# Holding the first products of the first gate stage in text order, and giving stored half tiles back later

## The chip, the cores and the metric

The kernel runs on one core of a Trainium2 chip. TensorE multiplies matrices into PSUM banks; VectorE and ScalarE do the elementwise work; GpSimd does a little of it and issues the stores of intermediate results; SyncE issues loads. Each engine works through its own list of instructions in order and waits at an instruction until what it depends on is done. The metric is the device time of one execution in microseconds (us); lower is better.

## The reference

One decoder layer with two recurrent branches on the same normalised input. For the change only its end matters: each branch output is projected, weighted by a sigmoid gate that comes from the input projection, and the sum goes through one output projection.

```python
proj = h @ w_in[l]
hq, hf, hi, hz, gq, gk, gv, gz, ga, mg = jnp.split(proj, IN_OFFSETS, axis=-1)
y_h = hgrn2_branch(hq, hf, hi, hz, lb_all[l], hgrn_norm_w[l])
y_g = gla_branch(gq, gk, gv, gz, ga, gla_alpha_w[l], gla_alpha_b[l], gla_norm_w[l])
u_h = y_h @ w_branch[l, 0]
u_g = y_g @ w_branch[l, 1]
mg = jax.nn.sigmoid(mg.reshape(B, T, N_BRANCH, D_MODEL))
merged = mg[:, :, 0] * u_h + mg[:, :, 1] * u_g
x = x + gate[:, None, :] * (merged @ w_out[l])
```

All of it is float32, 1024 rows by 1024 columns for `h`, each gate and each `u`.

## The kernel before

**The last stages.** The two gate projections and the two branch projections are four weight blocks b: 0 is the gate of the second branch (its sigmoid is `gate1`), 1 the other gate, 2 and 3 the branch projections. Each 1024 x 1024 product is cut into 2 x 2 blocks and computed with seven products of sums of blocks instead of eight (Strassen's way), in the order p = 1, 2, 5, 3, 6, 7, 4 (`PRODUCTS`). A product has four pairs i = 0 to 3 (two 128-row output tiles each), and for each pair `Pair.run` issues 12 matmuls (line 1343): four slices kt of the inner dimension times three terms n, since each float32 operand is split into a high and a low part. (b,p) i below is one such run. Its result stands in a PSUM bank of 512 columns.

**What each run needs and leaves.** The operands: a raw tile is loaded by SyncE (weights L1274 and L1278, inputs L1230), ScalarE makes the high part (L1285 for weights, L1263 or L1260 for inputs) and VectorE the low part (L1286, L1264, L1261). W(b,p,j) stands for the weights of pairs 2j and 2j+1, H(b,p) for the input side. After a run, `Pair.after` copies or combines banks: L1317 and L1315 copy a bank to a half tile in SBUF (`snap_of`), L1323 copies one back (`seed`), L1330 adds a copy and a bank on VectorE (`summed`), and `outs[b]` puts the finished half tile away. For b = 0 that is `put_gate1`: a sigmoid on ScalarE (L1414) and a store to DRAM on GpSimd (L1415); the gate is loaded again in the last two blocks. A new run into a bank waits for the copy that empties it.

**Slots.** All tiles of the last stages live in 46 slots of SBUF. `Slots` hands out the slot that has been free longest. `Halves` (called `Q`) cuts a slot into two halves of 128 x 512; a free half of a slot that is already open goes first. A tile that gets a slot waits until all that was done with its last owner is over, a store included.

**What sets the order.** Inside some stretches the order of instructions is the text's. Elsewhere, and in the whole of the stretch that the change touches, a list scheduler of the framework orders each engine's instructions by what depends on what and by its estimates; `tc.keep_in_program_order(m)` ties an instruction to the one ahead of it on its engine in the text. The first gate stage (b = 0) lies where the recurrent branches finish (L683 to L967: scores, decays, norms), so TensorE's rows of both are mixed.

Of the kernel before, what the change touches and what calls it, by code (L numbers as in the profile page):

```python
# [83 lines left out]
def hybrid_trunk_kernel(  # L84
# [6 lines left out]
    nc = tc.nc  # L91
# [10 lines left out]
    Q = Halves(S)  # L102
# [35 lines left out]
    def load_x(t):  # L138
        b = S.get([D])
        nc.sync.dma_start(b, x2[t * P:(t + 1) * P, :])  # L140
        return b
# [357 lines left out]
    for n in (1, 4):  # L499
        m = cp.tile([P, 8 // n, 6, n], F32, name=f"mask{n}")  # L500
# [6 lines left out]
    m = cp.tile([P, 1, 16], F32, name="mask16")  # L507
# [39 lines left out]
    class Feat:  # L547
# [12 lines left out]
        def run(self):  # L560
            ps = dtile()
            yield from mm_feat(self.wt, self.rhs, ps, self.w)
            S.free(*self.wt)
            self.done(ps)
# [742 lines left out]
    class Pair:  # L1307
# [25 lines left out]
        def run(self, p):  # L1333
            if p in (1, 5):
                self.bank[BANK[p]] = R.get()
            o = self.bank[BANK[p]]
            hi, lo = (z[:, self.i % 2, :] for z in wt[self.b, p, self.i // 2])
            h = H[0 if self.b == 1 else self.b, p]
            for kt in range(4):
                h_hi, h_lo = (z[kt // 2][:, kt % 2, :] for z in h)  # L1340
                sl = slice(kt * P, (kt + 1) * P)
                for n, (a, c) in enumerate(((hi, h_hi), (hi, h_lo), (lo, h_hi))):
                    nc.tensor.matmul(o, a[:, sl], c, start=(p in (1, 5) and kt == 0 and n == 0),  # L1343
                                     stop=(kt == 3 and n == 2), skip_group_check=True)
                if kt % 2:
                    stream.weave(1)
            if self.i % 2:
                S.free(*wt.pop((self.b, p, self.i // 2)))

        def after(self, p):  # L1350
            bank, snap, out = self.bank, self.snap, outs[self.b]
            if p == 1:
                if self.b:
                    self.seed()
                else:
                    snap[1] = self.snap_of("a", -1.0)
            elif p == 2:
                out(2 * self.i, 0, bank["a"], False)
                R.free(bank.pop("a"))
            elif p == 5:  # L1360
                snap[5] = self.snap_of("e")
            elif p == 6:
                snap[6] = self.snap_of("b", -1.0)
                self.summed(0, 1, None, bank["e"], ALU.subtract, 6)
                R.free(bank.pop("e"))
            elif p == 7:
                self.summed(1, 1, bank["b"], None, ALU.add, 5)
            elif p == 4:
                out(2 * self.i + 1, 0, bank["b"], False)
                R.free(bank.pop("b"))  # L1370
# [41 lines left out]
    def put_gate1(d, half, ap, summed):  # L1412
        g = ap if summed else Q.get()
        nc.scalar.activation(g, ap, AF.Sigmoid)  # L1414
        nc.gpsimd.dma_start(gate1_d[d][:, half * 512:half * 512 + 512], g)  # L1415
        Q.free(g)

    def put_gate0(d, half, ap, summed):
        nc.scalar.activation(merged(d, half), ap, AF.Sigmoid)
# [13 lines left out]
    def put_m(d, half, ap, summed):  # L1433
# [5 lines left out]
        if d % 2 != half:  # L1439
            S.free(gate1.pop(d))  # L1440

    outs[:] = [put_gate1, put_gate0, put_t1, put_m]


# [5 lines left out]
    for g in BUILT[1:]:  # L1450
        n = GROUPS.index(g)
# [53 lines left out]
    def load_rows(*ts):  # L1505
        for t in ts:
            xr[t] = load_x(t)

    bank4, snap4 = {}, {}

    def out_run(p, i):
# [141 lines left out]
    for b in (2, 3):  # L1653
        for p, i, z in ((3, 3, "11"), (6, 1, "21"), (6, 3, "12"), (7, 2, "22")):
            after(b - 1, p, i, lambda b=b, z=z: load_quad(b, z))
            if b == 3:
                p, i = {(3, 3): (7, 2), (6, 1): (7, 3), (6, 3): (4, 2), (7, 2): (4, 3)}[p, i]
# [61 lines left out]
```

## Time and profile before

| | |
|---|---|
| median of 3 runs | 1216.99 us (1215.41 to 1218.84) |
| profiled execution | 1216.46 us, span 1214.8 us |
| TensorE busy | 1184.1 us, 97% |
| VectorE, ScalarE, GpSimd busy | 65%, 45%, 10% |
| granted TensorE clock | 0.998 |
| first gate stage | about 806 to 900 us of the span |

The profile gives one execution on the chip. Its views used below: the page with the engines' busy shares; a table of busy time by stretches; each engine's own line of time (start, length, engine, line, tiles, count, and in brackets the idle time before the row and what ended it); the DMA groups with the time from issue to landing. Matmuls are pipelined: the length of a row of many says more than that of one. PE is TensorE, DVE is VectorE, ACT is ScalarE, POOL is GpSimd, SP or SPq is SyncE.

### The profile page before, as it was taken

How to read it: one execution, taken by the hardware profiler on the slowest of the kernel's cores; microseconds unless marked ns; L12 is line 12 of the kernel's file. 1: busy time of each engine (PE TensorE's matmuls, PEld its weight loads, DVE VectorE, ACT ScalarE, POOL GpSimd, SP SyncE). 2: the span in 40 equal slices, each digit the busy share in tenths (PEclk: the TensorE clock that was granted, in tenths of full speed). 3: DMA queues.
4: the chain of work that ended last, by engine and by line, in shares of the span. 5: the costliest groups of instructions: out<-in, count | busy, mean ns of one | idle time of the engine just before them, and what ended most of it. 6: DMA issues, size and time to landing. Idle time of an engine off the chain costs nothing.

```text
span 1214.8 us, 20860 instructions
## 1 busy us (share of the span) xinstructions
PE 1184.1 (97%) x8579; PEld 982.6 (81%) x8579; DVE 790.9 (65%) x1245; ACT 546.9 (45%) x797; POOL 123.8 (10%) x215
## 2 busy tenths in 40 slices
PE   5999999999999999999999999999999999999997
PEld 3777889889798888888887888877778888878886
DVE  4637444774848456877884365794653775988994
ACT  5646732434434244344332324455743544444554
POOL 4100000202111121121110101011220000000000
PEclk9999999999999999999999999999999999999999
DMA  9814000844444267255341112054697746435523
GB/s 320 277 70 139 18 19 19 293 141 161 156 152 149 66 207 249 94 179 169 108 174 47 59 53 70 36 174 158 227 343 277 260 160 208 135 104 173 174 104 122
DMA packets 130961, 183.51 MB, mean 151 GB/s; under 512 B 7467, under 2 KB 97633, under 8 KB 130866
## 3 DMA queue, kind: packets, MB, share of 16 engines
q1 hardware_dynamic: 117250, 136.87, 35.7%
q0 software_dynamic: 13568, 45.31, 9.6%
q8 instruction: 67, 1.10, 0.4%
q14 instruction: 28, 0.23, 0.1%
q10 hardware_dynamic: 48, 0.01, 0.0%
HBM read 132.87 MB, written 49.28 MB: 150 GB/s over the span
## 4 chain that ended last, share of the span: by engine, by line
PE 61%; issue 23%; DVE 3%; ACT 3%; POOL 2%; DMA 1%; POOLq 0%; ACTq 0%; DVEq 0%
PE pd L541 19%; PE pd L1343 9%; PE sc_ps L1343 5%; PE pm L1343 5%; PE pd L1520 3%; PE pd L643 2%; PE pd L644 2%; PE pd L645 2%; PE sc_ps L1520 2%; PE pm L848 1%; PE pd L352 1%; PE pm L829 1%; PE pm L850 1%; PE pm L1520 1%; PE sc_ps L352 1%
## 5 line engine op out<-in xcount | busy, mean ns | idle before, releaser
L541 PE MATMUL pd<-b,b 128*128 128x512 f32 x1632 | 387.4, 394 | 0.0
L541 PEld LDWEIGHTS pd<-b,b 128*128 128x128 f32 x1632 | 302.4, 188 | 64.8 <-issue 1.4
L1343 PE MATMUL pd<-b,b 128*128 128x512 f32 x720 | 173.7, 392 | 4.3 <-ACT b L1414 2.1
L1343 PEld LDWEIGHTS pd<-b,b 128*128 128x128 f32 x720 | 133.7, 188 | 35.7 <-ACT b L1414 3.2
L197 DVE TENSOR_TENSOR b<-b,b 128x1024 fp32r<-128x1024 f32 (+2 forms) x89 | 98.9, 1122 | 83.1 <-ACT b L196 65.4
L196 ACT CAST b<-b 128x1024 fp32r<-128x1024 f32 (+2 forms) x89 | 82.9, 948 | 92.1 <-DVE b L1199 14.6
L1286 DVE TENSOR_TENSOR b<-b,b 128x1024 fp32r<-128x1024 f32 x56 | 68.3, 1224 | 66.9 <-ACT b L1285 52.3
L1285 ACT CAST b<-b 128x1024 fp32r<-128x1024 f32 x56 | 58.3, 1050 | 73.9 <-PE pd L1343 20.6
L1343 PE MATMUL sc_ps<-b,b 128*128 128x512 f32 x324 | 79.4, 391 | 1.0 <-ACT scT L793 1.0
L600 PE MATMUL pd<-b,b 128*128 128x256 f32 x256 | 74.2, 290 | 0.0
L1264 DVE TENSOR_TENSOR b<-b,b 128x1024 fp32r<-128x1024 f32 x48 | 59.2, 1251 | 20.8 <-ACT b L1263 15.1
L602 PE MATMUL pd<-b,b 128*128 128x256 f32 x256 | 72.5, 283 | 0.0
L601 PE MATMUL pd<-b,b 128*128 128x256 f32 x256 | 72.4, 283 | 0.0
L1343 PEld LDWEIGHTS sc_ps<-b,b 128*128 128x128 f32 x324 | 60.3, 188 | 14.6 <-ACT scT L793 1.4
L1343 PE MATMUL pm<-b,b 128*128 128x512 f32 x300 | 72.1, 389 | 0.0
L1263 ACT CAST b<-b 128x1024 fp32r<-128x1024 f32 x48 | 49.9, 1050 | 41.2 <-PE pd L1343 16.0
L1343 PEld LDWEIGHTS pm<-b,b 128*128 128x128 f32 x300 | 56.3, 188 | 11.7
L352 PE MATMUL pd<-b,b 128*128 128x512 f32 x192 | 53.3, 410 | 2.0 <-ACT b L196 0.9
L1201 POOL DMA_DIRECT2D ws<-b x64 | 34.6, 541 | 192.0 <-DVE b L1195 86.5
L735 ACT COPY xb<-b 128x512 f32<-128x512 f32 x48 | 29.4, 620 | 49.4 <-PE sc_ps L715 26.7
L643 PE MATMUL pd<-b,b 128*128 128x512 f32 x128 | 51.3, 401 | 0.0
L644 PE MATMUL pd<-b,b 128*128 128x512 f32 x128 | 50.0, 390 | 0.0
(285 smaller groups left out, 1964.3 us busy)
## 6 DMA issues: line engine op xcount, KB each, us to landing
b<-in_w_in_dram SPq DMA_DIRECT2D x66, 512.0 KB, 4.2
ws<-b POOLq DMA_DIRECT2D x64, 256.0 KB, 3.3
b<-ws SPq DMA_DIRECT2D x32, 512.0 KB, 4.9
b<-in_x_dram SPq DMA_DIRECT2D x16, 512.0 KB, 5.7
b<-in_ada_w_dram SPq DMA_DIRECT2D x32, 256.0 KB, 6.9
b<-in_w_branch_dram SPq DMA_DIRECT2D x16, 512.0 KB, 4.4
b<-h SPq DMA_DIRECT2D x14, 512.0 KB, 4.3
wo<-b POOLq DMA_DIRECT2D x14, 512.0 KB, 5.7
```

What stands on the lines that cost most here:

```text
L196: nc.scalar.copy(hi, src)
L197: nc.vector.tensor_sub(lo, src, hi.bitcast(F32))
L352: nc.tensor.matmul(accs[f], wg(a, d, f), b[d][:, half * 512:half * 512 + 512], start=(d == 0 and n == 0), stop=(d == KT - 1 and n == 2))
L541: nc.tensor.matmul(ps[0:w, th * 512:(th + 1) * 512], a[:, k, 0:w], b[:, th * 512:(th + 1) * 512], start=(k == 0 and n == 0), stop=(k == KT ...
L600: nc.tensor.matmul(o, lh, hi[:, k % 4, :], start=(k == 0), stop=False)
L601: nc.tensor.matmul(o, lh, lo[:, k % 4, :], start=False, stop=False)
L602: nc.tensor.matmul(o, ll, hi[:, k % 4, :], start=False, stop=(k == KT - 1))
L643: nc.tensor.matmul(o, lh, hi[:, k % 2, :], start=(k == 0), stop=False)
L644: nc.tensor.matmul(o, lh, lo[:, k % 2, :], start=False, stop=False)
L1286: nc.vector.tensor_sub(lo, t, hi.bitcast(F32))
L1343: nc.tensor.matmul(o, a[:, sl], c, start=(p in (1, 5) and kt == 0 and n == 0), stop=(kt == 3 and n == 2), skip_group_check=True)
L1520: nc.tensor.matmul(o, a, b, start=(p in (1, 5) and kt == 0 and n == 0), stop=(kt == 3 and n == 2), skip_group_check=True)
```

## The change

For b = 0 and p = 1, the first matmul of each pair is tied to the matmul ahead of it in the text. And a half tile that `put_gate1` has stored is not freed at once: it goes into a list, and is freed when three newer ones stand behind it; the last three are freed after the run (1,2) i0.

```diff
@@ Pair.run
-                    nc.tensor.matmul(o, a[:, sl], c, start=(p in (1, 5) and kt == 0 and n == 0),
-                                     stop=(kt == 3 and n == 2), skip_group_check=True)
+                    m = nc.tensor.matmul(o, a[:, sl], c, start=(p in (1, 5) and kt == 0 and n == 0),
+                                         stop=(kt == 3 and n == 2), skip_group_check=True)
+                    if (self.b, p) == (0, 1) and kt == 0 and n == 0:
+                        tc.keep_in_program_order(m)
@@ put_gate1
         nc.gpsimd.dma_start(gate1_d[d][:, half * 512:half * 512 + 512], g)
-        Q.free(g)
+        sent.append(g)
+        drop_sent(3)
+
+    sent = deque()
+
+    def drop_sent(leave):
+        while len(sent) > leave:
+            Q.free(sent.popleft())
@@ ahead of the output stage
+    after(1, 2, 0, lambda: drop_sent(0))
```

Lines behind the first addition stand two further down in the new kernel, those behind the second nine and more: the sigmoid L1414 is L1416 there, the gate store L1415 is L1417.

The lists of instructions show what the scheduler makes of it; names of buffers carry a number. On TensorE, in (0,1), `pd_7440` is the bank of i0 and i1, `pd_7441` that of i2 and i3. What stood between i0 and i1:

```order
 L1343 MATMUL pd_7440<-b_7395,b_7404 128x512
 L1343 MATMUL pd_7440<-b_7393,b_7405 128x512
-L1343 MATMUL pd_7441<-b_7392,b_7442 128x512
-L1343 MATMUL pd_7441<-b_7394,b_7442 128x512
-L1343 MATMUL pd_7441<-b_7392,b_7443 128x512
-L1343 MATMUL pd_7441<-b_7392,b_7442 128x512
 L1343 MATMUL pd_7440<-b_7392,b_7404 128x512
 L1343 MATMUL pd_7440<-b_7394,b_7404 128x512
```

These four matmuls of i2 now stand behind the twelve of i1, with the other eight of i2; nothing of i2 is ahead of i1 any more.

On ScalarE, from (0,5) on. Before, `b_7887<-pd_7440` is the copy of the bank of (0,5) i2 (first row of that name) and L196 belongs to the last norm:

```order
L1315 COPY b_7821<-sc_ps 128x512
L1263 CAST b_7940<-b_7889 128x1024
L1315 COPY b_7887<-pd_7440 128x512
L196 CAST b_7906<-b_4458 128x1024
L1263 CAST b_8030<-b_7991 128x1024
L1285 CAST b_7972<-b_7870 128x1024
```

And now, where that copy is `b_7862<-pd_7440`:

```order
L1315 COPY b_7862<-sc_ps 128x512
L196 CAST b_7903<-b_4458 128x1024
L1285 CAST b_7911<-b_7805 128x1024
L1263 CAST b_7939<-b_7887 128x1024
L1315 COPY b_7862<-pd_7440 128x512
L1285 CAST b_7970<-b_7868 128x1024
```

L196, a weight cast and an input cast moved ahead of the copy.

On ScalarE again, at the last product (0,4). Before, `b_8233<-b_8159` is the cast of W(1,1,0), the sigmoids on `b_7887` are those of (0,7) i2 and i3, and `b_8215<-pd_7441` is that of (0,4) i0:

```order
L1285 CAST b_8196<-b_8110 128x1024
L1414 ACTIVATE b_7821<-b_7821 128x512
L1285 CAST b_8233<-b_8159 128x1024
L1414 ACTIVATE b_7887<-b_7887 128x512 x2
L1414 ACTIVATE b_8215<-pd_7441 128x512
L1285 CAST b_8270<-b_8200 128x1024
```

And now, where the cast of W(1,1,0) is `b_8225<-b_8153`:

```order
L1285 CAST b_8190<-b_8104 128x1024
L1416 ACTIVATE b_7862<-b_7862 128x512 x2
L1285 CAST b_8225<-b_8153 128x1024
L1416 ACTIVATE b_7907<-b_7907 128x512
L1416 ACTIVATE b_7907<-pd_7441 128x512
L1285 CAST b_8260<-b_8194 128x1024
```

Both orders have the cast ahead of the sigmoid of (0,4) i0; now it has one sigmoid fewer behind it, and the tile that this sigmoid writes is another.

On SyncE, the loads of raw weights at that place. Before, `b_8159` is the raw tile of W(1,1,0) and `b_8200` that of W(1,1,1):

```order
L1230 DMA b_8081<-fx_735 128x1024
L1278 DMA b_8110<-in_w_in_dram 128x4x128 x2
L1278 DMA b_8159<-in_w_in_dram 128x4x128 x2
L1278 DMA b_8200<-in_w_in_dram 128x4x128 x2
L1466 DMA b_8328<-in_w_out_dram 128x2x512
```

And now, where W(1,1,0) is `b_8153` and W(1,1,1) is `b_8194`:

```order
L1278 DMA b_8057<-in_w_in_dram 128x4x128 x2
L1278 DMA b_8104<-in_w_in_dram 128x4x128 x2
L1278 DMA b_8194<-in_w_in_dram 128x4x128 x2
L1278 DMA b_8153<-in_w_in_dram 128x4x128 x2
L1278 DMA b_8229<-in_w_in_dram 128x4x128 x2
```

The load of W(1,1,1) moved ahead of that of W(1,1,0), and its tile has the slot that holds two of the gate half tiles until their stores have landed.

## Prediction

> **What bounds the kernel now.** I read the page's share of busy time first, then a table of busy time by stretches over the first gate stage (the only place where the order of instructions changes, about 800 to 925 us), then each engine's own line of time there.
>
> Page, engine totals (busy us, share, instructions):
> ```profile
> PE 1184.1 (97%) x8579; PEld 982.6 (81%) x8579; DVE 790.9 (65%) x1245; ACT 546.9 (45%) x797; POOL 123.8 (10%) x215
> ```
> TensorE is 97% busy, so a change that issues the same matmuls can only win what TensorE idles and can only lose by new idling. Table by stretches of the first gate stage:
> ```profile
> core 0: us, PE busy (x) PEld busy (x) DVE busy (x) ACT busy (x) POOL busy (x), PEclk, DMA share, GB/s
> ...
> 870.00:893.00 23.00, 21.18 (x94) 17.13 (x93) 19.22 (x20) 13.07 (x19) 7.51 (x14) 1.00 0.89 303
> 893.00:906.00 13.00, 13.00 (x58) 10.75 (x59) 1.84 (x2) 3.84 (x6) 1.62 (x3) 1.00 1.02 352
> ```
> TensorE is short of full by 1.8 us from 870 to 893 and full behind it; the DMA share there is 0.89 and then 1.02, so transfers late in the stage land late. TensorE's line of time names each stall (start, length, line, tiles, count, idle before it and what ended that):
> ```profile
> 811.90 5.73 PE L1343 MATMUL pd<-b,b 128*128 128x512 f32 x24 [1.49 <-DVE b L953]
> ...
> 824.04 0.63 PE L770 MATMUL sc_ps<-xb 128*16 128x16 f32 x56
> ...
> 834.02 1.89 PE L1343 MATMUL sc_ps<-b,b 128*128 128x512 f32 x7 [0.96 <-ACT scT L793]
> 836.19 3.00 PE L1343 MATMUL pd<-b,b 128*128 128x512 f32 x12 [0.28 <-ACT b L1414]
> ...
> 854.39 0.40 PE L964 MATMUL pm<-b,ones_r 128*128 128x512 f32 x1
> ...
> 859.83 8.45 PE L1343 MATMUL pd<-b,b 128*128 128x512 f32 x36 [0.15 <-ACT b L1315]
> 868.12 1.07 PE L1343 MATMUL pm<-b,b 128*128 128x512 f32 x4
> 869.03 2.97 PE L1343 MATMUL pd<-b,b 128*128 128x512 f32 x12
> ...
> 889.98 1.07 PE L1343 MATMUL pm<-b,b 128*128 128x512 f32 x4
> 892.87 3.02 PE L1343 MATMUL pd<-b,b 128*128 128x512 f32 x12 [1.82 <-ACT b L1414]
> ```
> Five stalls: 1.49 + 0.96 + 0.28 + 0.15 + 1.82 = 4.70 us. One matmul costs (868.12 - 859.83) / 36 = 0.23 us. By starts the last stall is 892.87 - 889.98 - 4 x 0.23 = 1.97, 0.15 more than shown; with that for all five, 5.5 us. That is the most the change can gain, 0.45% of the span.
>
> I write (b,p) for product p of weight block b, i0 to i3 for its four pairs, and D for how late TensorE is in the changed kernel against the rows above.
>
> **The change, part by part.** The hold itself costs nothing on an engine: it adds an order and no instruction. But it, and the later freeing of half tiles, moves rows on TensorE, VectorE, ScalarE and SyncE, and each move is priced here. Rows of ScalarE and VectorE in the first part:
> ```profile
> 811.05 0.59 ACT L1317 ACTIVATE b<-pd 128x512 f32<-128x512 f32 x1
> ...
> 828.34 1.06 ACT L1260 ACTIVATE b<-b 128x1024 fp32r<-128x1024 f32 x1 [3.59 <-DMA gate<-b]
> ```
> ```profile
> 822.62 0.19 DVE L759 COPY_PREDICATED blk<-mask,sc_ps 128x32 f32<-128x32 int32 x1
> 822.72 1.22 DVE L1286 TENSOR_TENSOR b<-b,b 128x1024 fp32r<-128x1024 f32 x1
> 827.62 1.23 DVE L1261 SCALAR_TENSOR_TENSOR b<-b,b 128x1024 fp32r<-128x1024 f32 x1 [3.69 <-PE pd L1343]
> ```
> *(0,1).* Before, i2's first four matmuls stand ahead of i1 and wait for L953 until 811.9. Now i1 stands first and needs the bank copy L1317, which loses the L1260 ahead of it and can end at 811.05: i1 starts at 811.1, D = -0.8.
>
> *(0,2).* An L1286 (1.22) and an L1261 (1.23) now stand ahead of the last L759, so it ends near 822.81 + 2.45 - 0.69 (an L743 now behind it) = 824.5, and the score matmuls L770, which would be ready at 823.2, wait 1.2. Both L1260 (1.05 each) now stand ahead of the first sigmoid; i1 starts 0.7 later than before. The gain of the hold is spent there. The 0.96 and 0.28 stalls shrink, because TensorE has four matmuls fewer to fill with (0.9 us of work goes behind); by 836 I count D = 0, between -1 (the L1260s are hidden in TensorE's wait, as the 3.59 idle in the row of L1260 allows) and +1.
>
> *(0,5).* Rows from 845 to 855:
> ```profile
> 849.64 2.55 POOL L1107 TENSOR_TENSOR b<-b,b 128x1024 f32<-128x1024 f32 x1
> ```
> ```profile
> 852.22 1.05 ACT L196 CAST b<-b 128x1024 fp32r<-128x1024 f32 x1 [1.18 <-POOL b L1107]
> 853.18 1.04 ACT L1263 CAST b<-b 128x1024 fp32r<-128x1024 f32 x1
> ```
> Before, the copy L1315 of i2's bank stood ahead of L196, which waits for GpSimd's L1107. Now L196 and two casts stand ahead of that copy, and i3 waits for it. L1107 starts about 1 us earlier (its input comes after fewer matmuls), ends near 851.1; then L196, cast, cast at 0.96 from start to start (853.18 - 852.22) and the copy 0.58: i3 starts at 851.1 + 3 x 0.96 + 0.6 = 854.6. Its 12 matmuls end at 857.35, where before the row after them, the second norm matmul, stood at 854.62 (854.39 + 0.23): D = +2.7, and without the 0.3 stall at 859.83 +2.4. If L1107 came 2.1 us earlier still, this term would be zero; if no earlier than before, +3.5. I take +2.4.
>
> *(0,6).* i1 waits for the copy L1317 of i0's bank. Before, that copy ran at once:
> ```profile
> 868.32 0.60 ACT L1317 ACTIVATE b<-pd 128x512 f32<-128x512 f32 x1 [0.69 <-PE pd L1343]
> ```
> Now three more casts stand ahead of it (H(0,7) low half, W(0,7,1), H(0,4)), the last behind VectorE's split of W(0,7,0) near 871.4 by my count of L1286/L1264 rows in series. Cast and copy bring it to 873.0. TensorE arrives at 869.03 + 2.4 + 2 more matmuls (0.46) = 871.9: 1.1 more, D = +3.5. Bounds: nothing (casts done while TensorE was late) and 2.0 (two more casts).
>
> *(0,4).* The last stall has two sides. It went to a sigmoid whose half tile was still being stored:
> ```profile
> 889.35 1.05 ACT L1285 CAST b<-b 128x1024 fp32r<-128x1024 f32 x1 [2.33 <-DMA b<-in_w_in_dram]
> 890.31 1.14 ACT L1414 ACTIVATE b<-b 128x512 f32<-128x512 f32 x2
> 892.22 0.60 ACT L1414 ACTIVATE b<-pd 128x512 f32<-128x512 f32 x1 [0.76 <-DMA gate<-b]
> ```
> ```profile
> 881.74 0.54 POOL L1415 DMA_DIRECT2D gate<-b  x1 [1.26 <-ACT b L1414]
> ```
> ```profile
> b<-in_w_in_dram SPq DMA_DIRECT2D x12, 256.0 KB, 5.1
> ```
> (The last row is of the DMA view from 840 to 912 us: median us to landing.) With later freeing that 0.76 and the wait behind it go: the tile is another. But the cast L1285 of W(1,1,0) still stands ahead of the sigmoid of (0,4) i0, and its raw tile now loads on SyncE behind W(1,1,1)'s, whose tile is the slot of the stored halves of (0,6) i2 and i3: SyncE waits for that store to land, and with it everything queued behind. The store goes from GpSimd's 881.74 to about 883.8 (D less what its sigmoid's place gives), lands 4.6 later (median of all sixteen) at 888.4, the two pairs of loads take 0.5 us each to issue, so the fourth starts at 889.9 and lands 5.1 later at 895.0. Cast (0.96) and two sigmoids (1.14): 897.1. TensorE would arrive at 889.98 + 0.92 + 3.5 = 894.4 and waits 2.7 instead of 1.97: D = +4.2. The bounds are the shortest and longest landings of that store and those loads:
> ```profile
> DMA to landing us min/median/max: 2.3/4.6/8.3
> DMA to landing us min/median/max: 3.1/4.5/7.8
> ```
> (gate stores, then these loads.) Shortest, 4 us less: no wait, D = +1.5. Longest, about 6 us more: D = +10, which needs both extremes at once; one of them alone gives +7.
>
> *Behind 925 us* rows are in the same order on every engine; only the slots differ. TensorE is full there (the last row of the stretches), and I found no wait that a slot's new owner makes later by more than the slack it had, so D is carried to the end: TensorE's work is the end.
>
> **Sum.** 0 (up to 836) + 2.4 + 1.1 + (2.7 - 1.97) = +4.2 us. The profiled run before took 1216.46 with a span of 1214.8; the median of the three runs is 1216.99, 0.5 above. I carry the sum to the median: 1221.2.
>
> One place weighs a page against the rows. At the start of the span TensorE's line shows slow matmuls behind a stall of 3.99:
> ```profile
> 7.34 0.48 PE L219 MATMUL pm<-ident,b 128*128 128x128 f32 x1 [3.99 <-DVE b L210]
> 19.17 2.07 PE L352 MATMUL pd<-b,b 128*128 128x512 f32 x4 [0.20 <-ACT b L196]
> 24.45 1.21 PE L352 MATMUL pd<-b,b 128*128 128x512 f32 x4
> ```
> Four matmuls take 2.07 at 19.17 and 1.21 at 24.45; after the stall of 1.82 at 892.87 twelve take 3.02, which is full speed. So a stall between 1.82 and 3.99 us long may slow what follows. The Trainium skill, TensorE: Matmul & The Clock Gate, section Part 1: The HAM clock gate, says that TensorE falls to half its clock after an idle window of about 3.4 us and takes as long to come back. By that rule nothing is added to the forecast either, as its stalls are 2.7 at most, and the trace agrees so far; a longer one is the third rival below.
>
> **The rivals.** *The load is in time.* The store and loads of W(1,1,0) land as the shortest do, and the last stall is gone: D = 3.5 - 1.97 = +1.5, so 1218.5. For it: a store has landed in 2.3 and such a load in 3.1. Against it: the DMA share of 0.89 and 1.02 there. Chance 0.24.
>
> *The bank copies are not late (faster).* L1107 comes so early that L196 and the two casts end before i2's bank is full; it decides from L196 starting by about 849.0. Then (0,5) costs nothing, ScalarE is 2 to 3 us earlier through (0,6), the store goes out earlier too, and all five stalls go, 5.5, against the new 1.2 at L770 and 0.3 at the first sigmoid: -4.0, so 1213.0. For it: the 3.59 idle of ScalarE at L1260. Against it: L1107 waits for the two pm copies L1095, whose matmuls can't end 2 us earlier. Chance 0.10.
>
> *The clock drops.* If one of the stalls (2.3 at (0,5), 2.7 at (0,4)) grows towards the 3.99 of the row at 7.34, the matmuls behind it run as those at 19.17. They took 2.07 instead of 1.21, for 24.45 - 19.17 = 5.3 us at most: 5.3 x (1 - 1.21 / 2.07) = 2.2 more, on top of +5 (the stall itself 0.8 longer): 1224.2. Against it: it needs landings over the median. Chance 0.12.
>
> That the change does nothing is no rival: the rows of the four engines are in another order.
>
> **How the numbers follow.** Forecast (1219.5 to 1222.9 is its own range): 0.54. I call changes under 0.3% (3.65 us) no change, which a measurement of this kernel can hardly tell. Forecast and clock rival lie above 1220.64 with 0.41 + 0.12 = 0.53 (the forecast's low part, 0.13, lies below); the load in time lies within: 0.37; the early copies 0.10. The range leaves out half of the early copies and the extremes of the landings: 1215.5 to 1225.0.
>
> **What would show it.** In the profile after: TensorE's row of i1 of (0,1) starts near 811.1 without the wait for L953 (right); L770 waits for L759 by about 1.2; a stall before (0,5) i3 that ends with L1315, about 2.4; a stall before (0,6) i1 that ends with L1317; a stall of 2 to 4 us before (0,4) i1, ended by a sigmoid, while ScalarE waits for the load of W(1,1,0) and SyncE for a gate store. If the stall before (0,5) i3 is missing, the sum falls by 2.4; if SyncE doesn't wait for the gate store, by 0.7 to 2.7. A granted clock under 1.00 in the stretch from 893 to 906 would show the third rival. New idling after 925 us would make the whole prediction wrong.

## The result, and the profile after

The changed kernel takes 1221.12 us (median; 1216.95 to 1226.0) against 1216.24 for the kernel before (1214.69 to 1220.4): ratio 1.0032, 95% interval 1.0023 to 1.0041, which is 3.9 us slower (the medians lie 4.9 apart). The forecast was 1221.2. The profiled execution has a span of 1218.5 us against 1214.8. Its times spread more than those of before, and they go with the clock: of 18 executions, the eleven with a mean clock of 0.997 or less took 1220.1 to 1226.0, and five of the seven with 0.998 or more took 1217.0 to 1218.5 (the other two 1221.1 and 1221.7). Among the experiments below two executions, one of the later freeing with the tie and one with both ties, took 2158.9 and 1319.9 us at clocks of 0.77 and 0.85 and are left out of every number.

TensorE's line of time in the first gate stage, after:

```profile
810.92 5.73 PE L1343 MATMUL pd<-b,b 128*128 128x512 f32 x24 [0.69 <-ACT b L1317]
...
824.27 0.62 PE L770 MATMUL sc_ps<-xb 128*16 128x16 f32 x56 [1.14 <-DVE blk L759]
825.20 3.06 PE L1343 MATMUL pd<-b,b 128*128 128x512 f32 x12 [0.31 <-ACT b L1416]
...
835.02 3.00 PE L1343 MATMUL pd<-b,b 128*128 128x512 f32 x12 [0.74 <-ACT b L1416]
...
852.69 3.01 PE L1343 MATMUL pd<-b,b 128*128 128x512 f32 x12 [0.97 <-ACT b L1315]
855.54 0.39 PE L965 MATMUL pm<-b,ones_r 128*128 128x512 f32 x1
...
860.34 8.32 PE L1343 MATMUL pd<-b,b 128*128 128x512 f32 x36
...
871.37 3.01 PE L1343 MATMUL pd<-b,b 128*128 128x512 f32 x12 [1.35 <-ACT b L1317]
...
895.57 4.58 PE L1343 MATMUL pd<-b,b 128*128 128x512 f32 x12 [2.56 <-ACT b L1416]
900.00 4.70 PE L1343 MATMUL pm<-b,b 128*128 128x512 f32 x20
```

Seven stalls stand where five were, and the row at 895.57 is a surprise: from it to the next row twelve matmuls take 900.00 - 895.57 = 4.43 us, where twelve at 0.23 take 2.8. The table by stretches shows why (columns as in the table of before; the granted clock is the third number from the end):

```profile
893.00:895.50 2.50, 0.02 (x1) 0.00 (x0) 0.96 (x1) 2.04 (x4) 0.17 (x1) 1.00 1.05 404
895.50:899.00 3.50, 3.43 (x8) 2.75 (x9) 0.26 (x1) 1.68 (x3) 1.43 (x3) 0.51 1.06 382
899.00:906.00 7.00, 7.00 (x32) 5.79 (x32) 2.45 (x2) 1.52 (x3) 1.08 (x2) 1.00 0.98 332
```

Behind the stall TensorE ran at half clock for about 3.4 us. In the kernel before the stall of 1.82 at the same place left the clock at 1.00.

How late TensorE was against the kernel before, at the points of the prediction (work that stands on the other side of the point is taken off at 0.23 us a matmul):

| point | rows | D | this step | foretold |
|---|---|---|---|---|
| (0,2) i3 | 835.02 - 836.19 + 4 x 0.23 | -0.25 | -0.25 | 0 |
| (0,3) i2, behind (0,5) i3 | 860.34 - 859.83 | +0.51 | +0.8 | +2.4 |
| (0,6) i1 | 871.37 - 869.03 - 2 x 0.23 | +1.88 | +1.4 | +1.1 |
| (0,4) i1 | 895.57 - 892.87 | +2.70 | +0.8 | +0.7 |
| behind (0,4) i1 | 900.00 - 895.72 | +4.28 | +1.6 | 0 |

From there D is carried: the one later stall (0.47, by VectorE, 0.44 before) starts its matmuls at 1082.20 against 1078.06, and the last row of twelve matmuls stands at 1208.04 against 1203.96. The spans differ by 3.7.

### The profile page after: what moved, and what is told of

Same layout as the page of the kernel before. It is cut to its first block, busy times and chain, and to the rows that moved or that the text cites. A ratio compares the mean times of both kernels' runs of the same rounds, so it can differ in the third digit from the quotient of the medians.

```text
span 1218.5 us, 20859 instructions
## 1 busy us (share of the span) xinstructions
PE 1185.6 (97%) x8579; PEld 984.4 (81%) x8579; DVE 791.1 (65%) x1245; ACT 547.5 (45%) x797; POOL 122.4 (10%) x215
## 4 chain that ended last, share of the span: by engine, by line
PE 67%; issue 15%; DVE 5%; ACT 3%; DMA 2%; POOL 1%; SPq 0%; POOLq 0%; DVEq 0%; ACTq 0%
PE pd L541 22%; PE pd L1343 10%; PE sc_ps L1343 5%; PE pm L1343 5%; PE pd L1530 3%; PE pd L643 2%; PE pd L644 2%; PE pd L645 2%; PE pm L848 2%; PE sc_ps L1530 2%; PE pm L850 1%; PE pm L829 1%; PE pd L352 1%; PE pm L1530 1%; DMA b<-in_w_in_dram 1%
## 5 line engine op out<-in xcount | busy, mean ns | idle before, releaser
L1343 PE MATMUL pd<-b,b 128*128 128x512 f32 x720 | 174.5, 394 | 7.1 <-ACT b L1416 3.6
L1343 PEld LDWEIGHTS pd<-b,b 128*128 128x128 f32 x720 | 135.3, 189 | 38.6 <-ACT b L1416 4.5
L196 ACT CAST b<-b 128x1024 fp32r<-128x1024 f32 (+2 forms) x89 | 83.0, 948 | 94.4 <-DVE b L1199 14.7
L1286 DVE TENSOR_TENSOR b<-b,b 128x1024 fp32r<-128x1024 f32 x56 | 68.1, 1220 | 68.4 <-ACT b L1285 38.2
L1343 PE MATMUL sc_ps<-b,b 128*128 128x512 f32 x324 | 79.3, 392 | 0.0
L1343 PE MATMUL pm<-b,b 128*128 128x512 f32 x300 | 72.1, 389 | 0.0
L1343 PEld LDWEIGHTS sc_ps<-b,b 128*128 128x128 f32 x324 | 60.3, 188 | 13.0 <-DVE b L1444 0.3
L1343 PEld LDWEIGHTS pm<-b,b 128*128 128x128 f32 x300 | 56.3, 188 | 11.7
```

The costliest lines, as they stand in the source:

```text
L196: nc.scalar.copy(hi, src)
L1286: nc.vector.tensor_sub(lo, t, hi.bitcast(F32))
L1343: m = nc.tensor.matmul(o, a[:, sl], c, start=(p in (1, 5) and kt == 0 and n == 0), stop=(kt == 3 and n == 2), skip_group_check=True)
```

## The experiments

Theory A was that of the prediction: the later freeing moves casts and loads on ScalarE and SyncE ahead of what TensorE waits for, and the hold gains little. Rival B: the hold itself is what costs. Theory D came with the profile after: a stall costs its own length and then about 1.6 us more at half clock. Rival E: the slow stretch comes from the transfers.

Each experiment was run beside the kernel before, in one of three sets; the median of before is 1216.64 us in the first, 1215.71 in the second and 1215.88 in the third. Added lines shift the line numbers in the rows: L1416, L1418, L1419 and L1423 are the sigmoid L1414, L1323 is the copy L1315, L1347, L1350 and L1351 are the matmul L1343.

**The two halves apart.** The hold alone (half tiles are freed at once):

```diff
         sent.append(g)
-        drop_sent(3)
+        drop_sent(0)
...
-    after(1, 2, 0, lambda: drop_sent(0))
```

> The hold alone, half tiles freed at once as before. Its lists of instructions differ from before's only on TensorE: four matmuls of (0,1) i2 stand behind i1 instead of ahead of it. Theory A (the loss comes from the later freeing, which changes the lists of ScalarE, VectorE and SyncE): i1 starts when the copy L1317 ends, at 811.64 by before's row, 0.2 us earlier than the 811.90 of before, and the later stalls are those of before; 1216 us, ratio 0.999 to 1.000. Rival B (the hold causes the loss, since i2's four matmuls no longer fill a gap): 1219 to 1221, ratio 1.003.

Measured: 1216.59 us against 1216.64, ratio 1.000 (0.9991 to 1.0008). Two of its TensorE rows:

```profile
811.36 5.74 PE L1343 MATMUL pd<-b,b 128*128 128x512 f32 x24 [1.34 <-ACT b L1317]
...
892.27 3.01 PE L1343 MATMUL pd<-b,b 128*128 128x512 f32 x12 [1.46 <-ACT b L1416]
```

The wait for L953 turned into one for L1317 of nearly the same length, and the rest is as before. Rival B falls: alone, the hold is worth nothing.

The later freeing alone:

```diff
-                    if (self.b, p) == (0, 1) and kt == 0 and n == 0:
-                        tc.keep_in_program_order(m)
```

> The later freeing alone. Its lists are those of the changed kernel on every engine except for the four matmuls of (0,1) i2, which stand ahead of i1 as before. Theory A: the stalls before (0,5) i3, (0,6) i1 and (0,4) i1 are as in the changed kernel, and i2's first matmul waits for L953 until 812.8, 0.9 later than before, which the wait for L759 behind it hides to 0.6; 1221 to 1222 us, ratio 1.0035 to 1.005, a granted clock of 0.5 for some 3 us behind 895 in some executions. Rival B (the hold causes the loss): 1216 to 1217.

Measured: 1224.66 us against 1216.64, ratio 1.0058 (1.0037 to 1.0080), the mean clock of its executions 0.993 to 0.997. Its TensorE rows and the table by stretches:

```profile
812.10 5.69 PE L1343 MATMUL pd<-b,b 128*128 128x512 f32 x24 [2.72 <-DVE b L953]
...
852.40 3.01 PE L1343 MATMUL pd<-b,b 128*128 128x512 f32 x12 [0.97 <-ACT b L1315]
...
871.09 3.01 PE L1343 MATMUL pd<-b,b 128*128 128x512 f32 x12 [1.35 <-ACT b L1317]
...
894.67 4.60 PE L1343 MATMUL pd<-b,b 128*128 128x512 f32 x12 [1.94 <-ACT b L1414]
```

```profile
896.00:897.00 1.00, 1.00 (x3) 0.76 (x3) 0.00 (x0) 0.00 (x0) 0.03 (x1) 0.50 1.11 389
```

The later freeing brings the whole loss and more: the stalls of 0.97 in (0,5) and 1.35 in (0,6) again, 1.94 before (0,4) i1 with half clock behind it, and 2.72 for L953, which the later freeing makes later (it ends 4.2 us after TensorE's last row ahead of this stall starts, before 3.1). The kernel was slower than foretold by some 3 us. Its profile is the fastest of its six executions, 1219.6 us where the others take up to 1228.6, so it doesn't show where the rest goes; that stays open. The two halves don't add: 0 and +7 alone, +3.9 together.

**The last stall.** The changed kernel with one tie more: the cast of W(1,1,0) stays behind the sigmoids of (0,4) i0 and i1, where it stands in the text.

```diff
+    TIED = ((1, 1, 0),)
...
-        nc.scalar.copy(hi, t)
+        cast = nc.scalar.copy(hi, t)
+        if duo in TIED:
+            tc.keep_in_program_order(cast)
```

> The changed kernel with one more tie: the cast L1285 of W(1,1,0) stays behind the sigmoids of (0,4) i0 and i1, as in the text, so that no load stands between TensorE and the sigmoid that empties its bank. Theory A: the stall of 2.6 us before (0,4) i1 goes, and with it the stretch at half clock (1.6 us); what is left is the early part, which by then is 1.9 late against before less before's own stall of 1.97: 1216 to 1217 us, ratio 1.000 (0.9985 to 1.001), clock 0.998 or more, and the spread of the runs as narrow as before's. Rival C (TensorE is held at that place by the load of W(1,1,0) all the same, since (1,1) i0 needs it next): the stall moves to (1,1) i0, 1220 to 1221.

> The changed kernel with the tie on the cast of W(1,1,0) a second time, as the measure for the next two on the same chip: 1.0 to 1.5 us under before, ratio 0.9985 to 0.9992.

Measured: 1215.34 against 1216.64 (0.9988, 0.9979 to 0.9997), and in the third set 1215.18 against 1215.88 (0.9997, 0.9988 to 1.0006). The stall before (0,4) i1 is gone, and the stretch from 893 to 906 is full at full clock:

```profile
893.00:906.00 13.00, 13.00 (x59) 10.78 (x58) 3.67 (x3) 3.21 (x6) 1.08 (x2) 1.00 1.06 393
```

So the place of the cast that waits for its load is the cause of that stall, and the stall with the half clock behind it accounts for the change's loss: without it the changed kernel is as fast as before or slightly faster. Rival C (the stall moves to (1,1) i0) falls.

The same tie on the kernel before, without hold and later freeing:

> The kernel before with the tie on the cast of W(1,1,0) alone: no hold, half tiles freed at once. The lists differ from before's only in that cast and its VectorE half, two sigmoids later, and one GpSimd store. If the cast ahead of the sigmoid is what the last stall of before comes from, the stall of 1.82 before (0,4) i1 goes and nothing else changes: 1214.5 to 1215, ratio 0.9985. If it comes from the half tile that is still being stored (the profile names that wait, 0.76, behind the cast), part of it stays: 1216. Beside the changed kernel with the same tie (0.9988) it shows what the hold and the later freeing are worth once the load stands in nobody's way: equal, if the early stalls they remove and those they add weigh the same.

Measured: 1216.62 against 1215.71, ratio 1.0004 (0.9995 to 1.0012): nothing gained. ScalarE's row of the sigmoid of (0,4) i0 there, and TensorE's row that it releases:

```profile
893.30 3.03 PE L1347 MATMUL pd<-b,b 128*128 128x512 f32 x12 [1.70 <-ACT b L1418]
```

```profile
892.65 0.60 ACT L1418 ACTIVATE b<-pd 128x512 f32<-128x512 f32 x1 [1.60 <-DMA gate<-b]
```

The sigmoid no longer waits behind the cast, and then waits as long for the store of its half tile's last content; the stall of 1.82 is still 1.70. The last stall of before had two causes that end nearly together (in its profile the store's wait ends 0.76 us behind the cast and its sigmoids). The later freeing takes the store away, the tie the cast, and only both remove the stall.

**The stall before (0,6).** The changed kernel with the tie on W(1,1,0) and one on the input casts H(0,4):

```diff
+    TIED_H = ((0, 4),)
...
-                nc.scalar.copy(hi, src)
+                cast = nc.scalar.copy(hi, src)
+                if g in TIED_H:
+                    tc.keep_in_program_order(cast)
```

> The changed kernel with the tie on W(1,1,0) and one on the input casts H(0,4), which then stand behind the first sigmoid of (0,7) instead of ahead of the bank copy L1317 of (0,6) i0. If those casts are what holds that copy, the stall of 1.35 before (0,6) i1 goes: 1214 us, ratio 0.9975 to 0.998, unless (0,4) i0, which needs them, waits in its place by 0.5 to 1 (then 1215, as with the one tie). If the copy is late for another reason, the stall stays and the time is 1215.3.

> With the tie on H(0,4) too, a second time. Its profile has no stall before (0,6) i1 any more (1.35 with one tie), so it should stand 1.0 to 1.4 us under the run before it, ratio to before 0.997 to 0.998. If it is no faster than the run before it, the 1.35 us are given back somewhere that its one profile doesn't show.

Measured: 1214.86 against 1215.71 (0.9992, 0.9983 to 1.0000) and 1214.3 against 1215.88 (0.9987, 0.9978 to 0.9996). In the profile of the first the stall before (0,6) i1 is gone, none stands in its place, and the last one of the stage is this:

```profile
851.57 3.02 PE L1351 MATMUL pd<-b,b 128*128 128x512 f32 x12 [0.98 <-ACT b L1323]
```

The casts did hold that copy. But the time foretold, a ratio of 0.997 to 0.998, was missed both times. In the third set this kernel is 1.6 us under before and 0.9 under the run with one tie; over both sets its ratios of 0.9992 and 0.9987 aren't clearly under the 0.9988 and 0.9997 of one tie. What takes the rest of the 1.35 us is open.

**The clock.** The changed kernel with twelve matmuls that nobody reads, in a bank that is free, ahead of (0,4) i1:

```diff
+    FILL = 12
...
+            filler = (self.b, p, self.i) == (0, 4, 1)
+            if filler:
+                spare = R.free_list[0]
+                for _ in range(FILL):
+                    tc.keep_in_program_order(nc.tensor.matmul(
+                        spare, hi[:, 0:P], h[0][0][:, 0, :], start=True, stop=True, skip_group_check=True))
...
-                    if (self.b, p) == (0, 1) and kt == 0 and n == 0:
+                    if ((self.b, p) == (0, 1) or filler) and kt == 0 and n == 0:
```

> The changed kernel with 12 matmuls whose result nobody reads, into a bank that is free there, right ahead of (0,4) i1. They fill 2.8 us of TensorE's stall; four useful matmuls that stood there come 0.9 us later. Theory D (the stall costs its own length and then 1.6 us more, because TensorE runs at half clock for some 3.4 us behind a long stall): granted clock 1.00 from 893 to 906, no run with a clock under 0.998, and 2.7 + 0.9 = 3.6 us over before whatever the execution, 1219 to 1220, a spread as narrow as before's. Rival E (the slow stretch has another cause, such as the transfers of that stretch at a DMA share of 1.02): the stretch at half clock stays, 1221 to 1222, spread 1217 to 1226.

Measured: 1218.91 against 1216.64, ratio 1.0030 (1.0016 to 1.0043), eight of twelve executions from 1217.9 to 1219.4, four from 1221.9 to 1225.0. In its profile, an execution with late loads:

```profile
897.91 3.02 PE L1350 MATMUL pd<-b,b 128*128 128x512 f32 x12 [2.34 <-ACT b L1423]
```

```profile
893.00:906.00 13.00, 10.66 (x48) 8.49 (x47) 2.58 (x3) 5.25 (x7) 2.67 (x5) 1.00 0.94 344
```

The clock stays at 1.00 with the transfers at 0.94 of the DMA engines, which speaks against rival E, though the profile can't decide for theory D: its stall of 2.34 lies in two windows (last section), so no drop was due. The median is 0.1 us under the foretold 1219 to 1220, and eight of twelve executions are under the changed kernel's median by 1.7 us or more, although the kernel does more. Two things that theory D had foretold failed: the spread did not go, and two executions are at clocks of 0.996 and 0.997. Two of the four long executions are at clocks of 0.998 and 0.999, and in the profile, which is one of them, i1 starts 897.91 - 895.57 = 2.3 us later than in the changed kernel's; 0.75 of that stood already before (0,6) i1, the rest is the later landing of W(1,1,0)'s load (its cast waits 6.29 us for it, 4.71 in the changed kernel's).

The kernel before, with TensorE in text order in (0,4) and (1,1), so that the stall is in one piece:

```diff
-                    nc.tensor.matmul(o, a[:, sl], c, start=(p in (1, 5) and kt == 0 and n == 0),
+                    m = nc.tensor.matmul(o, a[:, sl], c, start=(p in (1, 5) and kt == 0 and n == 0),
...
+                    if (self.b, p) in ((0, 4), (1, 1)) and kt == 0 and n == 0:
+                        tc.keep_in_program_order(m)
```

> The kernel before with TensorE held in text order in (0,4) and (1,1): four matmuls that stood inside the stall before (0,4) i1 come behind it, so that TensorE idles 2.9 us there in one piece instead of 2.0. Theory D (a long stall is followed by about 3.4 us at half clock, 1.6 to 1.7 us lost, in those executions where it covers enough of a window): 0.9 over before and in some executions 1.6 more, 1217.5 to 1219, a clock of 0.996 or 0.997 in those. Rival E (the half clock comes from the transfers): 0.9 over before, no change of clock.

Measured: 1217.53 against 1215.71, ratio 1.0020 (1.0009 to 1.0031); five of ten executions at a clock of 0.996 or 0.997 (2.0 us longer on average), five at 0.998 or 0.999; of the kernel before ten of 29 are at 0.996 or 0.997 in this set. Its profile, one of the five at the higher clock, has a stall of 2.62 with the clock at 1.00:

```profile
892.90 3.01 PE L1343 MATMUL pd<-b,b 128*128 128x512 f32 x12 [2.62 <-ACT b L1416]
```

The same with six more sigmoids into the same half tile on ScalarE:

```diff
+        if (d, half) == (1, 0):
+            for _ in range(6):
+                nc.scalar.activation(g, ap, AF.Sigmoid)
         nc.scalar.activation(g, ap, AF.Sigmoid)
```

> As the run before it, with the sigmoid of (0,4) i0 computed six times more into the same half tile, 0.5 us each, so that TensorE idles about 6.0 us in one piece. Slots, loads and stores are those of before. Theory D: 0.9 + 3.1 us, and 1.7 more in every execution: 1222 to 1222.5, granted clock 0.5 for about 3.4 us behind the stall. Rival E: 1220.5, clock unchanged.

Measured: 1223.61 against 1215.71, ratio 1.0062 (1.0048 to 1.0076), clocks 0.992 to 0.996. TensorE's rows and the table by stretches:

```profile
898.01 5.49 PE L1343 MATMUL pd<-b,b 128*128 128x512 f32 x12 [6.33 <-ACT b L1419]
903.30 5.91 PE L1343 MATMUL pm<-b,b 128*128 128x512 f32 x24
```

```profile
893.00:896.00 3.00, 0.00 (x0) 0.00 (x0) 1.70 (x2) 2.91 (x6) 1.61 (x3) 0.61 1.01 365
896.00:898.00 2.00, 0.00 (x0) 0.00 (x0) 0.00 (x0) 1.87 (x4) 0.00 (x0) 0.50 1.05 424
...
901.00:902.00 1.00, 1.00 (x3) 0.73 (x3) 0.00 (x0) 0.00 (x0) 0.00 (x0) 0.50 1.07 328
902.00:904.00 2.00, 2.00 (x6) 1.58 (x5) 0.00 (x0) 0.09 (x1) 0.00 (x0) 0.53 0.42 122
904.00:910.00 6.00, 6.00 (x28) 4.93 (x27) 1.23 (x1) 3.60 (x5) 1.08 (x2) 1.00 0.34 99
```

The clock falls to half inside the stall, 2.0 us after TensorE went idle at 891.7: the trace's clock record has half clock from 893.64 to 903.88. Nothing was added on TensorE; twelve matmuls then take 5.29 us. Theory D's half clock is there, but the loss was larger than foretold, and at a transfer share of 1.01 this run alone doesn't exclude rival E. Behind the stall half clock lasted 5.9 us instead of the foretold 3.4, 1.2 us more lost. This profile also has half clock from 644.5 to 647.9 us, far from the edit.

**Hold and later freeing together.** The later freeing with the tie on W(1,1,0), without the hold:

```diff
-                    if (self.b, p) == (0, 1) and kt == 0 and n == 0:
-                        tc.keep_in_program_order(m)
```

> The later freeing with the tie on W(1,1,0), without the hold. Theory F (with the later freeing the hold is worth more than by itself, since L953 then comes 0.9 us later, i2's four matmuls would wait 2.9 us for it, and such a stall is followed by half clock in some executions): 0.5 to 2 us over the run with hold and tie, 1215.5 to 1217.5, clocks of 0.997 and less in part of the executions. Rival G (the 0.9 us are hidden in the later waits for L759 and L1315, and the excess of the later freeing alone came from its last stall): as the run with hold and tie, within 0.5.

Measured: 1218.1 against 1215.88, ratio 1.0015 (1.0006 to 1.0024), 0.0018 or 2.2 us over the run with hold and tie. TensorE's row of (0,1) i2 and the stretch behind it:

```profile
814.04 7.34 PE L1347 MATMUL pd<-b,b 128*128 128x512 f32 x24 [2.68 <-DVE b L953]
```

```profile
816.00:820.00 4.00, 4.00 (x13) 3.13 (x13) 3.23 (x11) 0.66 (x1) 0.00 (x0) 0.67 0.39 131
```

Twenty-four matmuls take 7.34 us, 1.6 more than the 5.73 of the same row in the changed kernel, and the transfers are at 0.39 there: half clock again, behind another stall. Theory F holds, though the time is 0.6 us above the foretold 1215.5 to 1217.5: the hold, worth nothing alone, is worth some 2 us once the later freeing has moved L953 back. It keeps a stall of 2.7 us down to 0.69 and avoids the half clock behind it (3.7 us together), and gives 1.4 of that back at L770 and the first sigmoid.

**The depth.** The changed kernel with one half tile held back instead of three:

```diff
-        drop_sent(3)
+        drop_sent(1)
```

> The changed kernel with half tiles given back one store later instead of three. On SyncE the load of W(1,1,0) is back ahead of that of W(1,1,1), and the cast W(1,1,0) has three sigmoids behind it before (0,4) i1 can start. If the loss of the change hangs on the place of that load (theory A), most of it goes: 1216 to 1218. If any later freeing costs the same, by the casts ahead of the copies in (0,5) and (0,6): 1220 to 1221.

Measured: 1221.79 against 1215.88, ratio 1.0045 (1.0031 to 1.0059). Its TensorE and ScalarE rows and the stretch behind:

```profile
814.96 7.33 PE L1343 MATMUL pd<-b,b 128*128 128x512 f32 x24 [3.12 <-ACT b L1317]
...
857.02 3.02 PE L1343 MATMUL pd<-b,b 128*128 128x512 f32 x12 [1.53 <-ACT b L1315]
...
888.29 3.01 PE L1343 MATMUL pd<-b,b 128*128 128x512 f32 x12 [1.80 <-DVE b L1330]
```

```profile
813.36 1.04 ACT L1285 CAST b<-b 128x1024 fp32r<-128x1024 f32 x1 [1.63 <-DMA b<-ws]
814.31 0.59 ACT L1317 ACTIVATE b<-pd 128x512 f32<-128x512 f32 x1
```

```profile
816.00:820.00 4.00, 4.00 (x13) 3.15 (x12) 3.21 (x8) 1.45 (x2) 0.00 (x0) 0.63 0.01 2
```

Theory A's number was wrong here. The stall before (0,4) i1 is gone, as it said; but another weight cast now stands ahead of the bank copy L1317 of (0,1) i0 and waits for its load, and the stall of 3.12 there takes the half clock with it. In that slow stretch, 815.5 to 819.0 us, the transfers are at 0.03 of the DMA engines, and in the kernel before and with the tie the clock was full at 1.02 and 1.06: with this rival E falls. A new stall of 1.80 also stands between (0,6) i1 and (0,4) i1, behind VectorE's L1330; no run tells its cause. So what the later freeing costs doesn't hang on one load's place: of the two depths tried, each gave the scheduler another order and put another cast that waits for its load ahead of a sigmoid or copy on which TensorE waits.

## Why the prediction was right or wrong

The time (1221.2 against 1221.12), the sign and the range were right, and the sum of 4.2 too (4.28 in the profile), but not all of its terms. That the times agree to 0.1 us is chance, as the changed kernel's executions spread over 9 us.

- *(0,1) and (0,2).* Right: i1 waits for L1317 (0.69), L770 waits 1.14 for L759 (foretold 1.2), 0.31 for the sigmoid, and by (0,2) i3 the hold's gain is spent (-0.25 against 0); of the stalls of 0.96 and 0.28 that were to shrink, one is gone and the other grew to 0.74.
- *(0,5).* The mechanism is there: i3 waits for L1315 behind L196 and two casts:

```profile
849.21 1.05 ACT L196 CAST b<-b 128x1024 fp32r<-128x1024 f32 x1 [1.15 <-POOL b L1107]
850.17 1.05 ACT L1285 CAST b<-b 128x1024 fp32r<-128x1024 f32 x1
851.12 1.04 ACT L1263 CAST b<-b 128x1024 fp32r<-128x1024 f32 x1
852.06 0.57 ACT L1315 COPY b<-pd 128x512 f32<-128x512 f32 x1
```

  The size failed, +0.8 against +2.4. The step that was wrong is "L1107 starts about 1 us earlier". It started 2.9 us earlier:

```profile
846.78 2.39 POOL L1107 TENSOR_TENSOR b<-b,b 128x1024 f32<-128x1024 f32 x1 [0.32 <-ACT b L1095]
```

TensorE came 1.2 us earlier to (0,2) i3 and had eight matmuls (1.8 us) fewer ahead of the rows that feed L1107's first inputs; I had counted most of these on the wrong side. By the prediction's own bounds (zero if 2.1 us earlier still) the 1.9 us more leave some 0.5, near the 0.8.
- *(0,6).* Right in place and cause (1.35 shown against 1.1), and the tie on H(0,4) showed the cause.
- *(0,4).* Right: ScalarE waits for the load of W(1,1,0), SyncE for a gate store, and TensorE for 2.56 (foretold 2.7). The cast and the waits that carry it, after:

```profile
893.46 1.04 ACT L1285 CAST b<-b 128x1024 fp32r<-128x1024 f32 x1 [4.71 <-DMA b<-in_w_in_dram]
```

```profile
SPq L1278 <- DMA gate<-b: 9.1, 2, 8.9
```

- *The clock.* Missing from the sum: +1.6. It stood among the rivals at a chance of 0.12, on the condition that a stall grow towards 3.99 us; 2.56 was enough. Its price, 2.2, was near the 1.6. The bound "between 1.82 and 3.99" was right and the value taken from it, the upper end, was not. The slow row at 19.17 can't carry that bound: the trace's clock record starts at 22.02 us, so TensorE may have been at half clock since the start, whatever the stall of 3.99. By the windows of the last section the foretold 2.7 us would halve the clock in about two of three executions (an estimate). The rule of the Trainium skill, TensorE: Matmul & The Clock Gate, section Part 1: The HAM clock gate, asks for an idle window of about 3.4 us. The length of the slow stretch here, 895.58 to 898.99, agrees with it, the length of the stall does not, and the measurement decides.

The 1.6 us too many at (0,5) and the 1.6 us missing for the clock cancelled. A reader who takes the sum as it stands is right by that accident; the experiments with the tie show that the stall before (0,4) i1 and the half clock behind it are what decides.

## What to carry to other kernels

A tile that is given back later changes more than its own waits: here it changed which slot later tiles get and, where a scheduler sets the order, the place of casts and loads. Look for the copy that frees the matmul engine's bank and for what stands ahead of it in its queue: a cast whose load is still on the way there costs what is left of the landing time (4.7 us of waiting on ScalarE here, 2.6 of them on TensorE), and one tie that kept the cast behind the sigmoids removed it. A wait with two causes that end together shows no gain until both are gone, so parts of a change must be tried together as well as apart.

## What the runs showed of the hardware

A stall of TensorE of 2 to 3 us can be followed by half clock for 3.41 us, 1.7 us of work lost; whether it is, the length of the stall alone doesn't say. The clock records of the traces, which give each change of the granted clock, say what does. In the changed kernel's profile it is full from 21.763 us, where the record starts, half from 895.575, full from 898.988 and half from 1213.014, behind the last matmul: 256, 1 and 92 times 3.41333 us apart. In thirteen profiles (all but that of the second run with both ties) the 29 intervals of this kind are all whole multiples of 3.41333 us, to a thousandth of that. So the clock changes only at the ends of windows of 3.41 us that run on their own, and what counts of a stall is its part in one window:

| run, stall | stall, us | most of it in one window | clock in the next window |
|---|---|---|---|
| before, (0,4) i1 | 1.82 | 1.37 | 1.00 |
| twelve more matmuls, (0,4) i1 | 2.34 | 1.73 | 1.00 |
| before with text order, (0,4) i1 | 2.62 | 1.76 | 1.00 |
| later freeing alone, L953 | 2.72 | 1.81 | 1.00 |
| later freeing alone, (0,4) i1 | 1.94 | 1.94 | 0.50 |
| six more sigmoids, first window | 6.33 | 1.95 | 0.50 |
| later freeing with the tie, L953 | 2.68 | 2.22 | 0.50 |
| the changed kernel, (0,4) i1 | 2.56 | 2.56 | 0.50 |
| one half tile held back, L1317 | 3.12 | 2.83 | 0.50 |

In these profiles up to 1.81 us of idle time in a window left the clock full, and 1.94 or more halved it. The windows lie elsewhere in each execution, and so one kernel has executions with and without the drop. As an estimate from these figures, a stall of 2.56 us has 1.94 or more in one window in (3.41 - 2.56 + 2 x 0.62) / 3.41 = 0.61 of all placements; eleven of the 18 executions of the changed kernel are at a clock of 0.997 or less. Behind the stall of 6.33 the clock stayed at half for a window that still held 0.96 us of it, and for the full one after that.

Three profiles (six more sigmoids, later freeing with the tie, one half tile held back) have a window at half clock near 644.5 to 648 us too, in rows that no edit touches. No idle time of TensorE is shown there; eight matmuls of L1062 and L1063 ahead of it take 4.1 us. So the length of one profile can hold 1.7 us that an edit has no part in.

Beside the hardware, the runs showed the size of an interaction: two edits worth 0 and +7 us alone were worth +3.9 together, and with one tie -0.4 to -1.5.
